# A transformer block in fp32 on TensorE: one section of the conditioning loaded earlier, block sums of the down projection split off and moved ahead, one gate/up operand made later, another order at the end

## The chip, the core and the metric

The kernel runs on one core of a Trainium2 chip. The metric is the device time of one execution in microseconds (us). Five engines work side by side, each through its own list of instructions in order: TensorE (PE, matrix products, with its weight loads as PEld), VectorE (DVE), ScalarE (ACT), GpSimd (POOL) and SyncE (SP), which here only issues DMA transfers. An instruction waits where its input is not there or its output buffer is still being read, and everything behind it on its engine waits too.

## What is computed

One block for a sequence of 1024 tokens of width 1024: a conditioning vector c gives six modulation sections; a normalised and modulated input goes through two kinds of attention, an output projection, a residual, a second modulated norm, a SwiGLU network of inner width 2816 and a last norm.

```python
mod = c_act @ w_ada[l] + b_ada[l]
sh_a, sc_a, g_a, sh_f, sc_f, g_f = jnp.split(mod[:, None, :], N_MOD, axis=-1)
h = rms_norm(x, g_mix[l]) * (1.0 + sc_a) + sh_a
x = x + g_a * hybrid_mixer(h, ...)
h = rms_norm(x, g_ffn[l]) * (1.0 + sc_f) + sh_f
x = x + g_f * swiglu(h, w_gate[l], w_up[l], w_down[l])
return rms_norm(x, g_final)
```

`swiglu` is `(silu(h @ w_gate) * (h @ w_up)) @ w_down`. The change touches the section sh_f (number 3 of six), the first block of gate/up, the down projection and the last norm.

## The kernel before

**Arithmetic.** Every fp32 product is made of three matrix products of two rounded parts: `split` (L160) lets ACT cast an operand to its high part (L162) and DVE subtract that from the operand, which is the low part (L158). In the trace these are `dhi`/`dlo`, `whi`/`wlo`, `ah`/`al`. Almost every subtraction of the kernel goes through the helper of L158, so operations are told apart by their tiles.

**Stages**, with the times at which they run in the profile: norm of x and the q/k/v projections up to 166 us; latent projections from 166 us on, and from 185 us the first attention steps between them; attention steps (`step`, the loop at L1223) to about 500 us; output projection and second norm to about 590 us; gate/up to 1022 us; down to 1243 us; the last evacuations and stores to 1255.3 us.

**What sets the order.** The code is written in the order in which each engine is to work; a scheduling layer moves instructions among their neighbours and then fixes each engine's list. Weights come through `Stream` objects (L57): an item is a load and a preparation; `pump` does the next preparation and issues loads a few items ahead, `need` and `ahead` pump up to a named item. Stream `st` feeds the stages up to the latents, `st2` output projection, gate/up and down. A third stream, `st3`, holds the eight items of section 3: each is a load of 512 KB (`adr`, L332) and one DVE operation of 128x1024 that multiplies by a number of c and accumulates (`acc`, L339 and L341); after the eighth, eight tiny matmuls (L373) turn the sum into columns, and DVE adds the bias (L383). The attention loop pumps one item of `st3` per step (L1225 to L1227). SP issues these loads in one queue with the attention's operands (`op`, L918 and L920). Working tiles share 49 slots of 4 KB per partition; a load waits in SP's queue until its slot is free.

**Gate/up** makes each block of 256 columns by seven products instead of eight (a Strassen form); `product` (L1333) is one of them, `half1` (L1280) and `rest` (L1298) make the activations' operands (`aop`: ACT cast, DVE low part) for products 6, 5, 3 and then 7, 4, and `fill` (L1331) lists what is still to be made during the first block. Operand 3 is made out of a PSUM tile, `psd`. Product 4 has weights of its own, `w4`, whose low part DVE makes last.

**Down** uses the same form over four quadrants in seven passes in the order 1, 2, 5, 6, 7, 3, 4 (`ORDER`). A pass goes through eleven items c = 0 to 10, each of 12 matmuls of 128x512 (three for each of four token tiles t). `dn_item` (L796) loads quarter blocks of g and of w_down and DVE prepares the operand: passes 1 and 2 take the blocks as they are; item ("5", c) first makes two block sums (L825 and the subtraction behind it, 128x512 each) into a tile `stt`, which passes 6, 3 and 4 use again. `ahead` (in the loop at L1469) keeps the preparations DLEAD = 3 items ahead of PE. `evac_dn` (L1419) adds a finished pass into the running results, `base21` (L1448) and `last21` (L1455) finish the last quadrant: for each t a multiplication with the gate (L1458), a subtraction from the residual x1, a square with its sum on ACT, the addition of two sums (L1462), POOL's reciprocal root (L221, L222), and the two scaled halves on ACT (L1464) and DVE (L1465), which are stored.

Of the kernel before, what the change touches and what calls it, by code (L numbers as in the profile page):

```python
# [12 lines left out]
P = 128  # L13
S = 1024
D = 1024
# [9 lines left out]
ALLOW = [(0, 'rope'), (12, ('qup', 2)), (25, None)]  # L25
# [28 lines left out]
DLEAD = 3  # L54
# [43 lines left out]
def emit(ctx, tc, a, out, dbg=None, rec=None):  # L98
# [12 lines left out]
    def slot(shape, dt, name):  # L111
        n = nm(name)
        if rec:
            rec.alloc(n)
        return sp.tile([P] + list(shape), dt, name=n, tag="s", bufs=NBUF)
# [284 lines left out]
    st.add("rope", load_tabs, lambda: None)  # L400
    for k in range(3):
        witem(st, ("qup", k), a["w_q_up"][k * P:(k + 1) * P, :], [768], nc.gpsimd)
    for k in range(2):
        witem(st, ("kvup", k), a["w_kv_up"][k * P:(k + 1) * P, :], [1024], nc.gpsimd)
    st3 = Stream(2)
    for it in col_sec(3, fin_shf):
        st3.add(*it)
# [388 lines left out]
    def dn_item(i, c):  # L796
# [5 lines left out]
        def dma():  # L802
            r = slot([2, 512], F32, "raw")
            q = None
            if i in "57":
                q = slot([2, 512], F32, "raw")
                if i == "5":
                    ld(out=r, in_=ga[:, :, HI].rearrange("f p t -> p f t"))
                    ld(out=q, in_=w0.rearrange("p (f n) -> p f n", f=2))
                else:  # L810
                    ld(out=r, in_=g0.rearrange("p (f n) -> p f n", f=2))
                    ld(out=q, in_=wa[:, :, HI].rearrange("f p t -> p f t"))
            else:
                x, y = {"1": (g0[:, LO], w0[:, LO]), "2": (g1[:, LO], w1[:, LO]), "6": (g0[:, LO], w1[:, HI]),
                        "3": (g1[:, LO], w1[:, HI]), "4": (g1[:, HI], w1[:, LO])}[i]
                ld(out=r[:, 0, :], in_=x)
                ld(out=r[:, 1, :], in_=y)
            raws[key] = (r, q)

        def prep():  # L820
            r, q = raws.pop(key)
            v = nc.vector
            if i == "5":
# [3 lines left out]
                r = z  # L827
# [81 lines left out]
    for i in ORDER:  # L909
        for c in range(NP):  # L910
            dn_item(i, c)

# [310 lines left out]
    for n in range(done, NS):  # L1223
        step(n, LA)
        if n > done:  # L1225
            st3.allow()
            st3.pump()  # L1227
        if n - NU in WOL:
            st2.need(("wo", WOL[n - NU]))
        for t in WOD.get(n - NU, []):  # L1230
            wout_d(t)
# [48 lines left out]
    def half1(jp):  # L1280
# [8 lines left out]
        if jp:  # L1289
            aop("5", jp, a11)  # L1290
        sub(nc.vector, a12, a22, a12)
        aop("3", jp, a22)
        sub(nc.gpsimd, a21, a21, t2)
        if not jp:
            aop("5", jp, a11)
# [35 lines left out]
    fill = [lambda: half1(0), lambda: half1(1)] + [lambda n=n, jp=jp: rest(n, jp) for n in "74" for jp in range(2)]  # L1331
# [123 lines left out]
    def last21(o, t):  # L1455
        t4 = 4 + t
        r = x1[t4]
        vtt(out=o, in0=o, in1=gf[:, LO], op=ALU.mult)  # L1458
        sub(nc.vector, r[:, LO], r[:, LO], o)
        sq(t4, LO, 0)  # L1460
        ss = ssq[t4]
        vtt(out=ss[:, 0:1], in0=ss[:, 0:1], in1=ss[:, 1:2], op=ALU.add)  # L1462
        rs = rstd_of(ss[:, 0:1], D)
        nc.scalar.activation(osl[t4][:, HI], r[:, HI], AF.Copy, scale=rs)  # L1464
        nc.vector.scalar_tensor_tensor(out=osl[t4][:, LO], in0=r[:, LO], scalar=rs, in1=gfin[:, LO], op0=ALU.mult, op1=ALU.mult)  # L1465
        for half in (HI, LO):
            ld(out=out[t4 * P:(t4 + 1) * P, half], in_=osl[t4][:, half])

    for n, i in enumerate(ORDER):  # L1469
# [7 lines left out]
        for c, t in seq:  # L1477
            if t == 0:
                ahead(("dn", i, c), DLEAD)
                if i in "17" and c in (2, 4, 6, 8):  # L1480
                    load_x1((c - 2) // 2 + (0 if i == "1" else 4))
# [16 lines left out]
    assert not pend  # L1498
# [54 lines left out]
```

## Time and profile before

| | us |
|---|---|
| three runs | 1255.12, 1257.43, 1259.67 (median 1257.43) |
| profiled execution | 1257.22 |
| its span | 1255.3 |
| PE busy in the span | 1205.8 (96%) |
| DVE busy | 829.2 (66%) |
| ACT busy | 494.4 (39%) |
| POOL busy | 439.0 (35%) |

The mean granted clock of TensorE was 0.983 of full speed. A row of the timeline gives the start, the duration, the engine, the line, the operation, out<-in, the shape, how many equal instructions it joins, and in brackets how long the engine sat idle before it and what ended that. A duration holds the engine's latency, so starts that follow each other without a wait are nearer together than durations: two operations of 128x512 on DVE that do not depend on each other start 0.60 us apart, though each is written as 0.68. In the page's slices 9 means nine tenths or more.

### The profile page before, as it was taken

The numbers are of one execution on the slowest core, as the hardware profiler recorded it, in microseconds if no ns is written. First come the engines' busy times: TensorE is split into PE (matmuls) and PEld (weight loads), VectorE is DVE, ScalarE is ACT, GpSimd is POOL, SyncE is SP. The second block draws the span as 40 slices with busy tenths as digits, with TensorE's granted clock in tenths as the row PEclk, the third lists the DMA queues.
The fourth block names the chain that finished last, engine by engine and source line by source line (L and its number), as shares of the span: only waits on it lengthen the run. The fifth ranks groups of instructions, "written<-read, shape, count | busy, mean of one in ns | idle before, by whom it ended". The sixth has DMA issues, their size and how long they took to land.

```text
span 1255.3 us, 16479 instructions
## 1 busy us (share of the span) xinstructions
PE 1205.8 (96%) x5951; PEld 1013.7 (81%) x5951; DVE 829.2 (66%) x1282; ACT 494.4 (39%) x850; POOL 439.0 (35%) x492
## 2 busy tenths in 40 slices
PE   8999999999899999999899999999999999999995
PEld 6888898988679898887688888878888888878774
DVE  6643514477697878768865565665555575699997
ACT  4542225455556665124532223313233244143353
POOL 4420002654243256113455445565444620000112
PEclk9999998999999999999899999999999999999998
DMA  9774842357986434321132233322122369779543
GB/s 369 301 255 167 313 137 74 106 170 227 336 250 166 137 109 144 116 94 59 51 118 96 91 117 125 110 84 84 51 101 84 117 234 393 250 252 327 190 129 135
DMA packets 82972, 209.33 MB, mean 167 GB/s; under 512 B 7805, under 2 KB 18379, under 8 KB 82763
## 3 DMA queue, kind: packets, MB, share of 16 engines
q1 hardware_dynamic: 63611, 168.36, 40.0%
q0 software_dynamic: 6336, 23.07, 4.8%
q10 hardware_dynamic: 12944, 16.84, 3.9%
q8 instruction: 47, 0.77, 0.2%
q14 instruction: 34, 0.28, 0.1%
HBM read 164.21 MB, written 44.04 MB: 166 GB/s over the span
## 4 chain that ended last, share of the span: by engine, by line
PE 77%; DVE 12%; ACT 4%; issue 4%; DMA 1%; POOL 1%; SPq 0%; ACTq 0%; POOLq 0%; DVEq 0%
PE psb L1338 32%; PE psb L439 5%; PE psb L441 5%; PE psb L440 5%; PE psb L481 3%; PE psd L481 3%; PE psd L1485 2%; PE psd L1486 2%; PE psd L1484 2%; PE psb L1030 2%; ACT s L949 2%; PE psb L1485 2%; PE psb L1484 2%; PE psb L1486 2%; DVE dlo L158 1%
## 5 line engine op out<-in xcount | busy, mean ns | idle before, releaser
L1338 PE MATMUL psb<-ah,whi 128*128 128x512 f32 x528 | 143.7, 394 | 2.9 <-ACT uv L1367 2.6
L1338 PE MATMUL psb<-ah,wlo 128*128 128x512 f32 x528 | 142.0, 391 | 0.8 <-DVE wlo L158 0.8
L1338 PE MATMUL psb<-al,whi 128*128 128x512 f32 x528 | 141.7, 390 | 0.4 <-DVE al L158 0.4
L1361 POOL TENSOR_TENSOR cf<-cf,cf 128x512 f32<-128x512 f32 x44 | 66.4, 1510 | 190.5 <-DVE cf L1354 183.9
L1338 PEld LDWEIGHTS psb<-ah,whi 128*128 128x128 f32 x528 | 99.3, 189 | 24.9 <-ACT uv L1367 3.0
L1354 DVE TENSOR_TENSOR cf<-psb,uv 128x512 f32<-128x512 f32 x88 | 60.3, 686 | 89.1 <-PE psb L1338 88.2
L1338 PEld LDWEIGHTS psb<-ah,wlo 128*128 128x128 f32 x528 | 99.6, 189 | 22.1 <-DVE wlo L158 1.2
L1338 PEld LDWEIGHTS psb<-al,whi 128*128 128x128 f32 x528 | 99.0, 188 | 21.4 <-DVE al L158 0.8
L162 ACT CAST whi<-ssum 128x1024 fp32r<-128x1024 f32 x44 | 45.0, 1045 | 166.9 <-POOL ssum L158 166.9
L158 DVE TENSOR_TENSOR wlo<-ssum,whi 128x1024 fp32r<-128x1024 f32 x44 | 62.3, 1416 | 55.5 <-ACT whi L162 55.5
L949 ACT ACTIVATE s<-s,nb 128x640 f32<-128x640 f32 (+7 forms) x96 | 74.4, 777 | 48.9 <-DVE nb L947 48.5
L162 ACT CAST dhi<-raw 128x1024 fp32r<-128x1024 f32 x63 | 64.5, 1051 | 64.5 <-DVE raw L158 29.0
L947 DVE CUSTOM_DVE_ANT_0 s<-psd,tabs 128x640 f32<-128x640 f32 (+7 forms) x80 | 63.3, 803 | 38.2 <-PE psd L973 36.1
L158 DVE TENSOR_TENSOR dlo<-raw,dhi 128x1024 fp32r<-128x1024 f32 x59 | 73.9, 1274 | 15.5 <-ACT dhi L162 15.3
L1485 PE MATMUL psb<-dlo,dhi 128*128 128x512 f32 x176 | 69.0, 392 | 0.1
L439 PE MATMUL psb<-whi,hh 128*128 128x512 f32 (+2 forms) x192 | 68.1, 354 | 1.0 <-ACT latq L638 0.9
L1486 PE MATMUL psb<-dhi,dlo 128*128 128x512 f32 x176 | 68.5, 389 | 0.0
L441 PE MATMUL psb<-whi,hl 128*128 128x512 f32 (+2 forms) x192 | 67.3, 350 | 0.0
L440 PE MATMUL psb<-wlo,hh 128*128 128x512 f32 (+2 forms) x192 | 67.2, 350 | 0.0
L1365 ACT ACTIVATE cf<-cf 128x512 f32<-128x512 f32 x44 | 27.8, 632 | 99.7 <-DVE cf L1354 99.7
L1484 PE MATMUL psb<-dhi 128*128 128x512 f32 x176 | 63.8, 391 | 1.1 <-ACT dhi L162 1.0
L1453 POOL TENSOR_TENSOR x<-x,gfin 128x512 f32<-128x512 f32 x4 | 5.5, 1377 | 164.3 <-ACT o L1417 160.0
(321 smaller groups left out, 3105.9 us busy)
## 6 DMA issues: line engine op xcount, KB each, us to landing
adr<-in_w_ada_dram SPq DMA_DIRECT2D x32, 512.0 KB, 6.4
raw<-scr_g SPq DMA_DIRECT2D x55, 256.0 KB, 3.6
raw<-in_w_down_dram SPq DMA_DIRECT2D x55, 256.0 KB, 4.2
raw<-in_w_gate_dram SPq DMA_DIRECT2D x22, 512.0 KB, 3.3
raw<-in_w_up_dram SPq DMA_DIRECT2D x22, 512.0 KB, 3.3
scr_g<-cf POOLq DMA_DIRECT2D x22, 512.0 KB, 3.2
raw<-scr_g SPq DMA_DIRECT2D x22, 512.0 KB, 5.4
raw<-in_w_down_dram SPq DMA_DIRECT2D x22, 512.0 KB, 6.2
```

The source lines that it names most:

```text
L158: pn(eng.tensor_tensor(out=o, in0=x, in1=y, op=ALU.subtract))
L162: pn(nc.scalar.copy(hi, raw))
L439: mm(o, lhsT=ah, rhs=bh, start=start, stop=False)
L440: mm(o, lhsT=ah, rhs=bl, start=False, stop=False)
L441: mm(o, lhsT=al, rhs=bh, start=False, stop=stop)
L481: pn(mm(o, lhsT=w[z == 2][:, m * 128:(m + 1) * 128], rhs=h[z == 1], start=(k == 0 and z == 0), stop=(k == 7 and z == 2)))
L949: nc.scalar.activation(s, s, AF.Exp, bias=nb[:, m:m + 1], scale=-1.0, accum_out=rs[:, m:m + 1])
L1338: mm(o, lhsT=w[l][:, k, :], rhs=x[2 * (k // 2) + r][:, k % 2, :], start=(l + r == 0 and k == 0), stop=(r == 1 and k == 3))
L1361: nc.gpsimd.tensor_tensor(out=g, in0=g, in1=o, op=ALU.mult)
L1484: mm(o[t], lhsT=hi[:, 0, tt], rhs=hi[:, 1, :], start=c == 0, stop=False)
L1485: mm(o[t], lhsT=hi[:, 0, tt], rhs=lo[:, 1, :], start=False, stop=False)
L1486: mm(o[t], lhsT=lo[:, 0, tt], rhs=hi[:, 1, :], start=False, stop=c == NP - 1)
```

## The change

1. Section 3 goes from `st3` into `st`, between the rope tables and the weights of the latents' up-projections; `st3` and its pumping are gone, and the first entry of `ALLOW` names the section's last item, so that all eight are pumped before and in the first latent projections.
2. The two block sums of down become items of their own, "s". Those of c = 0 to 5 stand after the items of passes 1 and 2 that `EARLY` names; the others directly ahead of ("5", c), which has no load of its own now. `DLEAD` is 5. The reloads of x1 go from passes 1 and 7 to passes 2 and 6.
3. In `last21` the DVE and ACT operations are pinned to the order of the code, and the second part of a tile (from the addition of the sums on) comes after the first part of the next tile.
4. In `half1` operand 5 follows operand 6 in both halves, and operand 3 is left to `fill`, which makes it after operand 7 and before operand 4.

```diff
-ALLOW = [(0, 'rope'), (12, ('qup', 2)), (25, None)]
+ALLOW = [(0, ('ad', 3, 7)), (12, ('qup', 2)), (25, None)]
...
-DLEAD = 3
+DLEAD = 5
+EARLY = [("1", 4), ("1", 7), ("1", 10), ("2", 2), ("2", 5), ("2", 8)]
...
     st.add("rope", load_tabs, lambda: None)
+    for it in col_sec(3, fin_shf):
+        st.add(*it)
     for k in range(3):
         witem(st, ("qup", k), a["w_q_up"][k * P:(k + 1) * P, :], [768], nc.gpsimd)
...
-    st3 = Stream(2)
-    for it in col_sec(3, fin_shf):
-        st3.add(*it)
...
         def dma():
+            if i == "5":
+                return
             r = slot([2, 512], F32, "raw")
             q = None
-            if i in "57":
+            if i in "s7":
...
-                if i == "5":
+                if i == "s":
                     ld(out=r, in_=ga[:, :, HI].rearrange("f p t -> p f t"))
                     ld(out=q, in_=w0.rearrange("p (f n) -> p f n", f=2))
...
-            if i == "5":
+            if i == "s":
                 z = stt[c] = slot([2, 512], F32, "stt")
                 v.tensor_tensor(out=z[:, 0, :], in0=r[:, 0, :], in1=r[:, 1, :], op=ALU.add)
                 sub(v, z[:, 1, :], q[:, 1, :], q[:, 0, :])
-                r = z
+                return
+            elif i == "5":
+                r = stt[c]
...
         for c in range(NP):
+            if i == "5" and c >= 6:
+                dn_item("s", c)
             dn_item(i, c)
+            if (i, c) in EARLY:
+                dn_item("s", EARLY.index((i, c)))
...
-        if n > done:
-            st3.allow()
-            st3.pump()
...
         aop("6", jp, t2)
-        if jp:
-            aop("5", jp, a11)
+        aop("5", jp, a11)
         sub(nc.vector, a12, a22, a12)
-        aop("3", jp, a22)
         sub(nc.gpsimd, a21, a21, t2)
-        if not jp:
-            aop("5", jp, a11)
+        sa["3", jp] = a22
         sa["4", jp] = a21
...
-    fill = [lambda: half1(0), lambda: half1(1)] + [lambda n=n, jp=jp: rest(n, jp) for n in "74" for jp in range(2)]
+    fill = [lambda: half1(0), lambda: half1(1)] + [lambda n=n, jp=jp: rest(n, jp) for n in "734" for jp in range(2)]
...
-        r = x1[t4]
-        vtt(out=o, in0=o, in1=gf[:, LO], op=ALU.mult)
-        sub(nc.vector, r[:, LO], r[:, LO], o)
-        sq(t4, LO, 0)
...
+        r, ss = x1[t4], ssq[t4]
+        pin(vtt(out=o, in0=o, in1=gf[:, LO], op=ALU.mult))
+        pin(vtt(out=r[:, LO], in0=r[:, LO], in1=o, op=ALU.subtract))
+        pin(nc.scalar.activation(osl[t4][:, LO], r[:, LO], AF.Square, accum_out=ss[:, 0:1]))
+        for fn in tail:
+            fn()
+
+        def rest():
+            pin(vtt(out=ss[:, 0:1], in0=ss[:, 0:1], in1=ss[:, 1:2], op=ALU.add))
+            rs = rstd_of(ss[:, 0:1], D)
+            pin(nc.scalar.activation(osl[t4][:, HI], r[:, HI], AF.Copy, scale=rs))
+            pin(nc.vector.scalar_tensor_tensor(out=osl[t4][:, LO], in0=r[:, LO], scalar=rs, in1=gfin[:, LO], op0=ALU.mult, op1=ALU.mult))
...
+        tail[:] = [rest]
...
-                if i in "17" and c in (2, 4, 6, 8):
-                    load_x1((c - 2) // 2 + (0 if i == "1" else 4))
+                if i in "26" and c in (2, 4, 6, 8):
+                    load_x1((c - 2) // 2 + (0 if i == "2" else 4))
```

The line numbers of the changed kernel are one higher near the top (L341 is L342), eight higher around L947 (now L955) and two higher in gate/up and down (L1354 is L1356, L1431 is L1433).

**Section 3 on DVE.** Before, among the attention steps; `ptl` is the low part of a transposed probability, the ISA operations are softmax's scaling:

```order
L341 SCALAR_TENSOR_TENSOR acc_3308<-adr_3310,cact,acc_3308 128x1024
L158 TENSOR_TENSOR ptl_3324<-psb_3381,pth_3323 128x4x128
L1000 RECIPROCAL rr_3316<-rs_3315 128x1
L158 TENSOR_TENSOR ptl_3342<-psb_3397,pth_3341 128x4x128
L1077 TENSOR_SCALAR ms_3414<-psb_3411 128x2
L341 SCALAR_TENSOR_TENSOR acc_3308<-adr_3312,cact,acc_3308 128x1024
L947 ISA s_3379,nb_3376<-psd_3390,tabs 128x768
L947 ISA nb_3376 128x1
L947 ISA s_3380,nb_3376<-psd_3404,tabs 128x768
```

In the change, behind the last low part of the values (`vl`) and ahead of the first softmax operation:

```order
L159 TENSOR_TENSOR vl_1322<-psb_1327,vh_1321 128x4x128
L340 TENSOR_SCALAR acc_1430<-adr_1388,cact 128x1024
L342 SCALAR_TENSOR_TENSOR acc_1430<-adr_1390,cact,acc_1430 128x1024
L342 SCALAR_TENSOR_TENSOR acc_1430<-adr_1392,cact,acc_1430 128x1024
L342 SCALAR_TENSOR_TENSOR acc_1430<-adr_1394,cact,acc_1430 128x1024
L342 SCALAR_TENSOR_TENSOR acc_1430<-adr_1432,cact,acc_1430 128x1024
L955 ISA s_1446,nb_1443<-psd_1447,tabs 128x128
L955 ISA nb_1443 128x1
```

Five of the eight accumulations stand together here; the other three follow in the next thirty rows.

**Gate/up, first block, on DVE.** Before, from the last low part of operand 3 (`al` out of `psd`) to w4:

```order
L158 TENSOR_TENSOR al_1293_6190<-psd_1286_6166,ah_1292_6189 128x1024
L1354 TENSOR_TENSOR cf_1280_6137<-psb_1294_6194,uv_1279_6136 128x512
L1354 TENSOR_TENSOR uv_1279_6136<-psb_1306_6245,uv_1279_6136 128x512
L158 TENSOR_TENSOR al_1296_6210<-ht_1268_6095,ah_1295_6209 128x1024
L1354 TENSOR_TENSOR uv_1279_6136<-psb_1307_6259,uv_1279_6136 128x512
L158 TENSOR_TENSOR al_1298_6214<-ht_1283_6153,ah_1297_6213 128x1024
L1354 TENSOR_TENSOR cf_1263_6075<-psb_1299_6217,uv_1262_6074 128x512
L158 TENSOR_TENSOR al_1301_6233<-ht_1229_5940,ah_1300_6232 128x1024
L158 TENSOR_TENSOR al_1303_6237<-ht_1254_6049,ah_1302_6236 128x1024
L158 TENSOR_TENSOR w4_1304_6240<-raw_1228_5938,w4_1304_6240 128x512
```

In the change, the same stretch:

```order
L1356 TENSOR_TENSOR cf_1278_6133<-psb_1290_6186,uv_1277_6132 128x512
L1356 TENSOR_TENSOR uv_1277_6132<-psb_1302_6237,uv_1277_6132 128x512
L159 TENSOR_TENSOR al_1292_6202<-ht_1268_6095,ah_1291_6201 128x1024
L1356 TENSOR_TENSOR uv_1277_6132<-psb_1303_6251,uv_1277_6132 128x512
L159 TENSOR_TENSOR al_1294_6206<-ht_1281_6149,ah_1293_6205 128x1024
L1356 TENSOR_TENSOR cf_1263_6075<-psb_1295_6209,uv_1262_6074 128x512
L159 TENSOR_TENSOR al_1297_6225<-psd_1271_6108,ah_1296_6224 128x1024
L159 TENSOR_TENSOR al_1299_6229<-psd_1284_6162,ah_1298_6228 128x1024
L159 TENSOR_TENSOR w4_1300_6232<-raw_1228_5938,w4_1300_6232 128x512
L159 TENSOR_TENSOR al_1305_6266<-ht_1229_5940,ah_1304_6265 128x1024
L159 TENSOR_TENSOR al_1307_6270<-ht_1254_6049,ah_1306_6269 128x1024
```

Operand 3's two low parts moved behind operand 7's, and operand 4's (from `ht`) from ahead of w4 to behind it.

**Down on DVE, ahead of the first evacuation of pass 7** (L1431, in the change L1433). `raw<-raw,stt` is the sum of an item of pass 3, the `dlo` of the same `raw` its low part. Before:

```order
L158 TENSOR_TENSOR raw_1969_10162<-raw_1970_10163 128x512
L158 TENSOR_TENSOR raw_1973_10186<-raw_1973_10186,stt_1844_9506 128x512
L158 TENSOR_TENSOR dlo_1976_10206<-raw_1960_10112,dhi_1975_10205 128x1024
L158 TENSOR_TENSOR dlo_1979_10227<-raw_1964_10136,dhi_1978_10226 128x1024
L158 TENSOR_TENSOR raw_1977_10209<-raw_1977_10209,stt_1849_9529 128x512
L158 TENSOR_TENSOR raw_1980_10230<-raw_1980_10230,stt_1854_9552 128x512
L158 TENSOR_TENSOR dlo_1983_10250<-raw_1969_10162,dhi_1982_10249 128x1024
L158 TENSOR_TENSOR dlo_1986_10270<-raw_1973_10186,dhi_1985_10269 128x1024
L1431 TENSOR_TENSOR uw_1766_9112<-psb_1950_10078,uw_1766_9112 128x512
```

In the change:

```order
L159 TENSOR_TENSOR dlo_1987_10248<-raw_1976_10164,dhi_1986_10247 128x1024
L159 TENSOR_TENSOR raw_1982_10210<-raw_1982_10210,stt_1808_9282 128x512
L159 TENSOR_TENSOR dlo_1990_10268<-raw_1979_10187,dhi_1989_10267 128x1024
L159 TENSOR_TENSOR raw_1985_10231<-raw_1985_10231,stt_1820_9346 128x512
L159 TENSOR_TENSOR dlo_1993_10288<-raw_1982_10210,dhi_1992_10287 128x1024
L159 TENSOR_TENSOR raw_1988_10251<-raw_1988_10251,stt_1834_9414 128x512
L159 TENSOR_TENSOR dlo_1996_10308<-raw_1985_10231,dhi_1995_10307 128x1024
L159 TENSOR_TENSOR raw_1991_10271<-raw_1991_10271,stt_1847_9481 128x512
L159 TENSOR_TENSOR dlo_1999_10328<-raw_1988_10251,dhi_1998_10327 128x1024
L1433 TENSOR_TENSOR uw_1767_9113<-psb_1962_10106,uw_1767_9113 128x512
```

One operand of pass 3 is finished ahead of the evacuation before the change, five are in the change.

## Rows read from the trace of the kernel before

**Rows 1.** The page's section 2: the span in 40 equal slices, in tenths

```profile
PE   8999999999899999999899999999999999999995
...
DVE  6643514477697878768865565665555575699997
...
PEclk9999998999999999999899999999999999999998
```

**Rows 2.** Waits of PE, longest in total: line <- releaser, us, times, longest

```profile
PE psb L988 <- DVE ptl L158: 4.2, 2, 4.0
...
PE psb L1338 <- ACT uv L1367: 2.6, 1, 2.6
...
PE psb L1338 <- DVE w L158: 2.3, 1, 2.3
```

**Rows 3.** The chain of waits, 318 to 380 us: start us, us, what

```profile
336.13 7.17 DMA adr<-in_w_ada_dram
...
343.39 1.06 DVE acc L341
...
345.33 0.69 PE psb L988
```

**Rows 4.** The timeline of SP's queue, 328 to 352 us: start, us, what

```profile
328.36 9.55 SPq L332 DMA_DIRECT2D adr<-in_w_ada_dram  x4
...
338.07 0.33 SPq L920 DMA_DIRECT2D op<-scr_qn  x1
```

**Rows 5.** The timeline of DVE, 140 to 200 us: ..., [idle before <- releaser]

```profile
166.31 0.69 DVE L158 TENSOR_TENSOR vl<-psb,vh 128x512 fp32r<-128x512 f32 x1 [4.75 <-ACT vh L459]
...
185.64 0.29 DVE L947 CUSTOM_DVE_ANT_0 s<-psd,tabs 128x128 f32<-128x128 f32 x1 [18.65 <-PE psd L973]
```

**Rows 6.** The timeline of PE, 598 to 628 us, product 4 of gate/up

```profile
622.10 1.92 PE L1338 MATMUL psb<-ah,w 128*128 128x512 f32 x4 [2.32 <-DVE w L158]
623.81 1.91 PE L1338 MATMUL psb<-al,w 128*128 128x512 f32 x4
```

**Rows 7.** The timeline of DVE, 596 to 624 us

```profile
611.13 1.21 DVE L158 TENSOR_TENSOR al<-psd,ah 128x1024 fp32r<-128x1024 f32 x1
...
616.93 3.44 DVE L158 TENSOR_TENSOR al<-ht,ah 128x1024 fp32r<-128x1024 f32 x2
...
620.29 1.75 DVE L158 TENSOR_TENSOR w<-raw,w 128x512 fp32r<-128x512 f32 x1
```

**Rows 8.** The timeline of DVE in the down projection, windows from 1078 to 1256 us

```profile
1081.58 0.70 DVE L1423 TENSOR_TENSOR psd<-psd,uw 128x512 f32<-128x512 f32 x1 [8.15 <-PE psd L1486]
1082.32 0.70 DVE L1410 TENSOR_TENSOR psd<-psd,gbc 128x512 f32<-128x512 f32 x1
...
1142.31 0.69 DVE L1428 TENSOR_TENSOR uw<-psd,uw 128x512 f32<-128x512 f32 x1 [2.00 <-PE psd L1486]
...
1172.02 0.69 DVE L1431 TENSOR_TENSOR uw<-psb,uw 128x512 f32<-128x512 f32 x1 [1.86 <-PE psb L1486]
...
1236.85 2.36 DVE L158 TENSOR_TENSOR dlo<-raw,dhi 128x1024 fp32r<-128x1024 f32 x2 [0.55 <-ACT dhi L162]
...
1240.26 1.30 DVE L1458 TENSOR_TENSOR psb<-psb,gbc 128x512 f32<-128x512 f32 x2 [1.05 <-PE psb L1486]
```

**Rows 9.** Windows: from:to, us, each engine's busy us (instructions), PEclk, DMA share, GB/s

```profile
340.00:350.00 10.00, 5.42 (x27) 5.01 (x28) 6.61 (x11) 2.99 (x8) 2.94 (x6) 0.66 1.02 404
...
1030.00:1080.00 50.00, 50.00 (x222) 41.43 (x221) 25.70 (x26) 18.14 (x20) 0.00 (x0) 1.00 1.00 368
...
1190.00:1200.00 10.00, 6.08 (x23) 3.92 (x22) 10.00 (x12) 5.07 (x7) 2.46 (x2) 0.96 0.36 117
```

**Rows 10.** The timeline of DVE at the end

```profile
1249.26 0.15 DVE L1462 TENSOR_TENSOR ssall<-ssall 128x1 f32<-128x1 f32 x1
1250.35 0.75 DVE L1465 SCALAR_TENSOR_TENSOR o<-x,rstd,gfin 128x512 f32<-128x512 f32 x1 [0.94 <-POOL rstd L222]
```

More of the change, by code (lines that the diff above doesn't have):

```diff
@@ L820, in prep @@
         def prep():
-            r, q = raws.pop(key)
+            r, q = raws.pop(key, (None, None))
             v = nc.vector
-            if i == "5":
+            if i == "s":
                 z = stt[c] = slot([2, 512], F32, "stt")
@@ L1456, in last21 @@
         t4 = 4 + t
-        r = x1[t4]
-        vtt(out=o, in0=o, in1=gf[:, LO], op=ALU.mult)
-        sub(nc.vector, r[:, LO], r[:, LO], o)
-        sq(t4, LO, 0)
[L1461 to L1467, printed above, removed]
+        r, ss = x1[t4], ssq[t4]
[9 more added lines that the diff above has]
+            pin(nc.vector.scalar_tensor_tensor(out=osl[t4][:, LO], in0=r[:, LO], scalar=rs, in1=gfin[:, LO], op0=ALU.mult, op1=ALU.mult))
+            for half in (HI, LO):
+                ld(out=out[t4 * P:(t4 + 1) * P, half], in_=osl[t4][:, half])
+        tail[:] = [rest]
+    tail = []
     for n, i in enumerate(ORDER):
@@ L1497, in emit @@
             pend += [lambda t=t: base21(t) for t in range(4)]
-    assert not pend
+    for fn in tail:
+        fn()
 _INS = ["x", "vecs", "ident", "ada_a", "ada_b", "w_ada", "b_ada", "w_in", "rope", "w_q_up", "w_kv_up", "tabs", "lam", "w_out",
```

## The prediction

> **What bounds the kernel now.** I read the page's slices first: PE stands at 9 tenths in nearly all of them, so a change pays only where PE has a hole. The holes, beside the start, are slice 11 (an 8: 314 to 345 us, attention), slice 20 (596 to 628 us, start of gate/up, with an 8 in the granted clock too) and the last; ahead of the last, DVE stands at 9 in four slices [rows 1]. The list of PE's waits then names who ends the holes: 4.2 us behind a DVE subtraction in the attention, 2.6 and 2.3 us in product line L1338 [rows 2]. Each of the four parts of the change has one of these places, and each was read in its own timeline.
>
> **Part 1, section 3.** In the chain of waits a load of `adr` runs 7.17 us, DVE's accumulation follows for 1.06, and then PE starts at 345.33 [rows 3]. PE had waited 4.0 us there [rows 2]. Nothing that PE computes at that place needs section 3: the accumulation only stands ahead of the low part of a probability in DVE's list, and DVE waits for the load. The window from 340 to 350 shows PE busy 5.42 us at a mean clock of 0.66, so part of the matmuls ran at the lower of the two levels (1.2 GHz for 2.4), with DMA at 1.02 [rows 9]. In SP's queue four `adr` loads stand from 328.36 on, over 9.55 us, ahead of an attention operand issued at 338.07 [rows 4].
>
> With the section gone from here, DVE goes straight on to the low part. The wait of 4.0 us goes, and 0.6 more of small gaps around it: -4.6. The clock: the 5.4 busy us at 0.66 would be some 3.6 at full clock, -1.9. The accumulations (eight, by the row of 1.06 some 8.5 us of DVE) are on the path only where DVE is late for PE; I estimate nothing beyond that. **-6.5**; bounds -2 (the next operand, late on a full DMA, takes over half of the wait) and -10 (4.6, 1.9 and three of the accumulations on the path).
> After a wait, PE's clock fell here: that the window stands at 0.66 is the row. The Trainium skill, "TensorE: Matmul & The Clock Gate", Part 1, says that the gate follows how busy PE has lately been, at two ratios only. By that the slow stretch stays if smaller gaps remain around the place, and the sum would be 1.9 us less negative; I take the full 1.9 since the gaps that remain are under 0.6.
>
> In its new place: DVE is idle 18.65 us up to 185.64, after the last `vl` at 166.31 [rows 5]. Five accumulations of 1.06 go there; the loads before it take slots that the first attention operands had, and these take slots which the values' projection frees from 170 on. That is over 10 us before the first softmax row, and a load took 7.17 at the worst place. Of the last three, one stands inside the first softmax chain: at most 1.06 to PE. Two stand in idle time. **+0.5**; bounds 0 and +3 (all three on the path).
>
> **Part 4, gate/up.** PE waits 2.32 us for w4's low part at 622.10, and the eight matmuls that follow start over 1.71 us per four [rows 6], where the first attention-free stretch (1030 to 1080: 222 in 50 us) gives 0.90 [rows 9]. DVE is without a gap before: the pair of low parts of product 4 takes 3.44 and w4 1.75, to 622.0 [rows 7]. The change puts that pair behind w4. Operand 3's two (1.21 each [rows 7]) stay ahead of w4 but leave the early part. So w4's low part ends about 3.4 us earlier, and PE needs it 2.3 earlier: the wait goes, -2.3. The pair that is now late is wanted after eight matmuls (1.8 us) and after ten; DVE gives it 1.2 and 2.4 us after w4: no new wait, with little to spare. The slow clock after the wait costs 2 x (1.71 - 0.90) = 1.6; I count none of it, since waits of some tenths remain around. Taking one cast of operand 3 (1.0 us, as long as the others) from ahead of ACT's copy `uv`, on which PE waits 2.6 [rows 2], gives 1.0. **-3.3**; bounds -1 (the copy alone) and -5 (with the clock).
>
> **Part 2, down.** In passes 6, 7 and 3 DVE has two sums and a low part per item. From 1190 to 1200 DVE is busy 10.00 us and PE 6.08 [rows 9]. A pass without waits takes 1172.02 - 1142.31 = 29.7 us [rows 8]; three more would end at 1231.4, but DVE's last pair of low parts starts at 1236.85 and ends at 1239.2, and PE's first result for the end comes at 1240.26 [rows 8]. So DVE sets the end, and what counts is the DVE work between 1142.31 and 1239.2 and DVE's gaps there. The gaps: 1.86 at 1172.02, where DVE waits for PE to end pass 7 with more operands to prepare behind the evacuation; 0.55 at 1236.85 [rows 8]; 1.22 of the same kind at the end of pass 3 by its timeline: 3.6. In the change five operands of pass 3 are ready ahead of that evacuation instead of one (the order above). DVE has then about 35 us of work from 1142.31 to there where PE needs 29.7, arrives after PE, and does not wait. The work: counting the rows from the first evacuation of pass 6 to the last low part in both orders, at 0.60 for an operation of 128x512 and 1.14 for a low part, 1.9 us less stand there in the change, since some were done before. **-5.4**; bounds 0 (DVE finds other gaps of the same size) and -7.8, at which PE's own 1231.4 is the limit.
>
> The cover for what moves earlier: from 1030 to 1080 DVE is busy 25.7 of 50 us [rows 9], and at 1081.58 it idles 8.15 us [rows 8]. The early sums are 6 x 1.2 = 7.2 us of DVE and 6 MB of loads in a stretch where DMA is full (1.00, 368 GB/s [rows 9]): 16 us of DMA. This window alone moved 18.4 MB. Passes 1 and 2 (22 items of 0.5 MB), the early sums, x1 (2 MB) and g_final (0.5) need 19.5 MB in all by 1081, and DLEAD lets at least five operands (2.5 MB) come before pass 1 starts, so the loads should still be ahead of PE. The x1 reloads move by a pass and cost nothing while that holds.
>
> **Part 3, the end.** Before, from 1240.26 to the end of the last row, 1250.35 + 0.75 = 1251.1: 10.8 us. Each tile needs the addition of sums, POOL's two operations and the last multiplication: 1249.26 to 1250.35, 1.09 us, in which DVE idles 0.94 [rows 10]. Before, DVE has another tile's operations in two of these four times. In the change the list reads mult, subtract (twice), then sum, multiplication, mult, subtract, sum, multiplication and so on: the sum and the multiplication that waits for it stand next to each other in all four tiles, with nothing between. A dependent pair starts 0.74 apart (1081.58 to 1082.32 [rows 8]), an independent one 0.60. So: 4 x (0.74 + 0.60) + 4 x 1.09 + 4 x 0.67 = 12.4. **+1.6**; bounds -1 (the first tile starts early, beside PE's last matmuls) and +2.5.
> The Trainium skill, "VectorE: DVE Perf Modes", The DRAIN you can't avoid, says the next operation waits for the pipeline to empty in any case, so that order among DVE operations would cost nothing; the two pitches of this trace differ, by 0.14. By the rule the end would be 4 x 0.14 = 0.6 shorter.
>
> **Sum**: -6.5 + 0.5 - 3.3 - 5.4 + 1.6 = -13.1, from the profiled execution's 1257.22: 1244.1. That execution stood 0.2 below the median of the runs, so 1244.3 against 1257.43. A difference of 0.3% (3.8 us) is about what can be told here from no change.
>
> **Rivals.**
> (a) *The attention gives little back.* DMA is full at 340 to 350 (1.02 [rows 9]); the attention operand behind the `adr` loads [rows 4] is late itself, PE waits for it, and the clock falls again. For: DMA share. Against: without 4 MB of `adr` (11 us at 368 GB/s) the operands come earlier. Then part 1 is worth -2, and the total -8.6: 1248.8.
> (b) *Down is not shortened.* DVE's gaps go, but ACT's casts, which end the gap at 1236.85 [rows 8], or the shorter lead of loads make others. Then -5.4 becomes 0, with +1.6 at the end: -7.7, 1249.7. With (a) too: 1254.
> (c) *Slower: the early sums' loads starve PE.* In the full-DMA stretch 1030 to 1080 up to six MB come ahead of pass 2's operands. If the loads are not ahead of PE as I think, PE stops in passes 2 and 5 for up to 16 us, plus some at the lower clock (as at 622.10, 1.6 each time): 16 + 3, against -13.1 + 5.4 from the rest: +11, about 1269. It decides whether the operands of pass 2 are prepared before PE comes to them; the 8.15 us of idle DVE [rows 8] speak against it.
> (d) *The change does not do what it says*: the layer that orders instructions undoes parts of it. The order shows section 3, w4 and the sums moved, so only the end (pinned) and the clock could be empty; within the range.
>
> **How the numbers follow.** The forecast's case, 1239 to 1247, has 0.58; (a) or (b) alone, 1247 to 1253, 0.24; both or smaller gains, 1253 to 1261, 0.10; (c) 0.07; the rest, faster than 1239, is 0.01. Faster by over 0.3% (below 1253.6): 0.84; within: 0.09; slower: 0.07. The range reaches from 1238 (part 1 and part 4 at their ends) to 1253 (a or b).
>
> **What would show it.** Right: no accumulation on DVE between 320 and 380, and PE's line L988 gone from its waits; five accumulations in the idle time before the first softmax row; product 4 without its wait; DVE without a gap over 0.6 from the evacuation of pass 6 to the last low part, with that low part about 5 us earlier against the start of pass 1; about 12.4 us from the first operation of the end to the last. Wrong: PE waits at DMA's operands in the attention at the same place; PE's waits in pass 2 or 5; a wait for w4's neighbours, `al` of product 4.

## The result

The changed kernel takes 1245.01 us (median of four runs, 1243.9 to 1246.36), the one before, run beside it, 1256.28 (1254.55 to 1259.67). The ratio is 0.9908, 95% interval 0.9882 to 0.9933: faster by 0.7 to 1.2%. Forecast were 1244.3 and a range of 1238 to 1253.

The page's slices of the changed kernel, in the order of [rows 1]:

```profile
PE   8999998999999999999899999999999999999994
...
DVE  6642625567777878768965565655555567598997
...
PEclk8999999999999999999999999999999999999997
```

The 8 of PE in slice 11 is gone; a new one stands in slice 7 (187 to 218 us, the latents with the first attention steps). Slice 20 keeps its 8, with the clock at 9 tenths now. The waits of PE, as in [rows 2]:

```profile
PE psd L980 <- DVE nb L955: 3.3, 4, 2.1
PE psb L1340 <- DVE al L159: 2.5, 3, 1.5
...
PE psb L1340 <- ACT ah L163: 1.8, 1, 1.8
...
PE psb L1340 <- ACT uv L1369: 1.4, 1, 1.4
```

The 4.2 us behind a probability's low part are gone; 0.9 us remain in all waits for such parts. In their place PE waits 3.3 us for softmax's scaling (L955), 3.0 of them at the first scores, and in gate/up the 2.3 us at w4 became 2.5 at low parts of activations.

To place the gain, I took from PE's and DVE's timelines the start of each stage's first matmul and the end of DVE's last operations, and compared the lengths between them. Each column below is one profiled execution, as a difference from the one of before; p1 to p4 are experiments that have one part of the change alone.

| stretch | changed | p1 | p2 | p3 | p4 |
|---|---|---|---|---|---|
| start to first q/k matmul | +1.9 | +1.8 | +1.5 | -0.2 | +1.3 |
| q/k to first `dv` matmul | 0.0 | 0.0 | +1.4 | 0.0 | +1.4 |
| to the first E by E score product | +1.5 | +1.6 | -2.6 | -2.5 | -2.7 |
| to the last E by E score product | -8.9 | -8.8 | +1.1 | +1.2 | -1.2 |
| to the first matmul of gate/up | 0.0 | 0.0 | -1.6 | 0.0 | 0.0 |
| gate/up | -1.1 | 0.0 | -0.2 | 0.0 | -0.9 |
| down, to the end of DVE's last low part | -6.3 | 0.0 | -6.3 | 0.0 | -1.3 |
| from there to DVE's last operation | +1.7 | 0.0 | +0.1 | +1.6 | 0.0 |
| span | -11.3 | -5.7 | -6.7 | +0.1 | -3.5 |

The E by E products are those of L988, the first of which follows the latents and the last of which lies in the attention. In the first rows also p2 to p4 differ, which do not touch those stages: there the same instructions take up to 2.7 us more or less by chance. In these profiles the rows of gate/up and of the end repeat to 0.3 us, and so does down but for p4.

### The profile page after: what moved, and what is told of

Same layout as the page of the kernel before. It is cut to its first block, busy times and chain, and to the rows that moved or that the text cites. A ratio compares the mean times of both kernels' runs of the same rounds, so it can differ in the third digit from the quotient of the medians.

```text
span 1244.0 us, 16493 instructions
## 1 busy us (share of the span) xinstructions
PE 1198.6 (96%) x5951; PEld 1011.3 (81%) x5951; DVE 828.8 (67%) x1282; ACT 495.5 (40%) x850; POOL 438.1 (35%) x492
## 4 chain that ended last, share of the span: by engine, by line
PE 79%; DVE 12%; issue 3%; ACT 3%; DMA 1%; POOL 1%; SPq 0%; ACTq 0%; POOLq 0%; DVEq 0%
PE psb L1340 32%; PE psb L439 5%; PE psb L441 5%; PE psb L440 5%; PE psb L481 3%; PE psd L481 3%; PE psb L1493 2%; PE psb L1494 2%; PE psb L1492 2%; PE psb L1038 2%; DVE dlo L159 2%; PE psd L1494 2%; PE psd L1493 2%; PE psd L1492 2%; ACT s L957 1%
## 5 line engine op out<-in xcount | busy, mean ns | idle before, releaser
L1356 DVE TENSOR_TENSOR cf<-psb,uv 128x512 f32<-128x512 f32 x88 | 60.3, 686 | 91.2 <-PE psb L1340 90.2
L955 DVE CUSTOM_DVE_ANT_0 s<-psd,tabs 128x640 f32<-128x640 f32 (+7 forms) x80 | 63.3, 804 | 28.6 <-PE psd L981 26.8
```

## Experiments

**One part alone**, each on the kernel before.

```diff
# p1_section: part 1
+    for it in col_sec(3, fin_shf):
+        st.add(*it)
...
# p2_down: part 2
+DLEAD = 5
+EARLY = [("1", 4), ("1", 7), ("1", 10), ("2", 2), ("2", 5), ("2", 8)]
...
# p3_end: part 3
...
+        tail[:] = [rest]
# p4_gate: part 4
+        aop("5", jp, a11)
...
+        sa["3", jp] = a22
...
```

> The kernel before with part 1 alone (section 3 loaded ahead of the latent up-projections). Theory: the attention gets shorter by 8.9 us between its first score product of the second kind and its last score, as between the two traces, and the latents longer by 1.4: about 7.5 us less than before. Rival: the accumulations' new place costs as much as the prediction's upper bound, or the attention's gain needs the other parts: 2 to 4 us less.

Measured: 1250.34 us, ratio 0.9956 (0.9939 to 0.9972). -8.8 in the attention and +1.6 ahead of it, as in the changed kernel: by the profiles the theory holds, and the rest of the change has no part in it. The medians differ by 4.9 us only (interval 3.5 to 7.7); what may lie between is told under no_section.

> The kernel before with part 2 alone (block sums as items, six of them early, five items of lead, x1 reloads in passes 2 and 6), old end. Theory: DVE without gaps after pass 6, last matmul 7.8 us earlier against the first of down: about 7.8 us less than before. Rival: the old end, whose DVE operations are mixed with the last preparations, loses as much as it gains: 3 to 5 us less.

Measured: 1250.17 us, ratio 0.9952 (0.9931 to 0.9972). The last matmul comes 7.8 us earlier against the first of down, as the theory says, but DVE's last low part, from which the end follows, only 6.3: PE finishes 2.2 us after that low part where it took 3.7. So the stretch that counts is 6.3 us shorter. The medians differ by 5.1 us, with an interval of 3.5 to 8.7 that holds theory and rival.

> The kernel before with part 3 alone (the pinned order at the end). Theory: DVE waits for POOL's two operations four times instead of two and a half: from the first operation of the end to the last 12.5 us instead of 10.8, about 1.6 us more than before. Rival: the new order is what lets the last matmuls end earlier against DVE's last low part (2.3 us instead of 3.8 between the two traces): no change, or 1 us less.

Measured: 1257.37 us, ratio 1.0014 (0.9994 to 1.0034). The runs cannot tell it from no change; the profile can: 1.6 us more between DVE's last low part and its last operation, and no other stretch that the part touches differs.

> The kernel before with part 4 alone (operand 3 made later). Theory: DVE is the bound in the first block of gate/up, and product 4 waits for its own low parts in place of w4: 1 to 1.3 us less than before, as between the two traces. The prediction's step: 3.3 us less.

Measured: 1252.97 us, ratio 0.9976 (0.9956 to 0.9996). Gate/up is 0.9 us shorter, 1.1 in the changed kernel: by the profiles the theory, not the prediction's 3.3; the interval of the runs, 0.5 to 5.5 us, holds both. (Of the 3.5 us of its span, the rest lies in stretches it does not touch.)

**The end in other orders**, on the changed kernel.

```diff
# old_end: the end as before
-        pin(vtt(out=o, in0=o, in1=gf[:, LO], op=ALU.mult))
+        vtt(out=o, in0=o, in1=gf[:, LO], op=ALU.mult)
...
# new_end: a tile's sum, then its scaled halves, each one tile later
-        for fn in tail:
-            fn()
...
+        if len(tail) == 2:
+            tail.pop(0)()
+        if tail:
+            tail[0] = tail[0]()
+        tail.append(total)
...
```

> The changed kernel with the old end (parts 1, 2 and 4). Theory: the pinned end costs 1.6 us here too, as when it stood alone: 1.6 us less than the changed kernel. Rival: with part 2 the old end's operations collide with the last preparations, and the pinned end is needed: no difference, or slower than the changed kernel.

Measured: 1243.39 us (1242.95 to 1245.69), ratio 0.9903 (0.9877 to 0.9928); the profile has 1.6 us less than the changed kernel in the stretch of the end, and the same down (-6.3). By the profile the theory holds; by the runs the interval overlaps with the changed kernel's.

> The changed kernel with a third order at the end: a tile's sum goes to POOL after the next tile's first part, and its scaled halves come after the first part of the tile after that, so that POOL's 1.1 us lie beside DVE's work. Theory: POOL's way is what the end waits for; from the first operation of the end to the last some 9.4 us where the changed kernel takes 12.5 and the one before 10.8: 3 us less than the changed kernel. Rival: the end is bound by ACT's squares and copies: 1 us less at most.

Measured: 1242.61 us (1242.32 to 1244.45), ratio 0.9896 (0.9872 to 0.9921). DVE's timeline at the end:

```profile
1228.35 0.69 DVE L1460 TENSOR_TENSOR psb<-psb,gbc 128x512 f32<-128x512 f32 x1
...
1231.01 0.15 DVE L1465 TENSOR_TENSOR ssall<-ssall 128x1 f32<-128x1 f32 x1
1231.08 0.69 DVE L1460 TENSOR_TENSOR psb<-psb,gbc 128x512 f32<-128x512 f32 x1
...
1232.41 0.74 DVE L1470 SCALAR_TENSOR_TENSOR o<-x,rstd,gfin 128x512 f32<-128x512 f32 x1
...
1236.24 0.75 DVE L1470 SCALAR_TENSOR_TENSOR o<-x,rstd,gfin 128x512 f32<-128x512 f32 x1 [0.73 <-POOL rstd L223]
1237.71 0.75 DVE L1470 SCALAR_TENSOR_TENSOR o<-x,rstd,gfin 128x512 f32<-128x512 f32 x1 [0.72 <-POOL rstd L223]
```

10.1 us from the first row to the end of the last, against 12.5 in the changed kernel and 10.8 before. The multiplication at 1232.41 follows its sum without a wait, because another tile's first part lies between; only the last two wait for POOL. Expected were 9.4: the third and fourth sums stand together, and POOL works them off one after the other. The interval of the runs overlaps with the changed kernel's here too.

**Section 3 in and out of its new place**, on the changed kernel.

```diff
# late_three
-ALLOW = [(0, ('ad', 3, 7)), (12, ('qup', 2)), (25, None)]
+ALLOW = [(0, ('ad', 3, 4)), (6, ('ad', 3, 7)), (12, ('qup', 2)), (25, None)]
# no_section
-ALLOW = [(0, ('ad', 3, 7)), (12, ('qup', 2)), (25, None)]
+ALLOW = [(0, 'rope'), (12, ('qup', 2)), (25, None)]
...
-    for it in col_sec(3, fin_shf):
-        st.add(*it)
+    nc.vector.tensor_copy(fcol[:, 1, :], V[:, 32:40])
```

> The changed kernel with the last three items of section 3 allowed six steps later, so that their accumulations stand behind the first unit's softmax instead of inside it. Theory: these three, each 1.28 us on DVE, keep back the first scores, on which PE waits 3.3 us in the changed kernel: from the values' projection to the first score of the second kind 2 to 4 us less, the attention unchanged. Rival: the latents' longer time comes from the order of the score products themselves or from the clock, not from these three: no difference.

Measured: 1244.91 us (1244.31 to 1246.09), ratio 0.9913 (0.9892 to 0.9935): the changed kernel's time. In the profile the stretch up to the first E by E product is 1.2 us longer than in the changed kernel and the attention 1.3 shorter. The accumulations did hold PE up: between 186 and 222 us it waits 1.3 us behind L955 where it waited 3.0. But its wait for ACT's `latq` at L669, 0.3 us in the changed kernel, is 2.1 now, so that its waits in that stretch come to 3.9 against 3.8, and the clock stood lower than the changed kernel's 0.88 (below):

```profile
186.00:200.00 14.00, 11.23 (x51) 9.78 (x50) 7.83 (x26) 8.23 (x24) 2.10 (x7) 0.76 0.14 38
```

So the theory falls as to what the move is worth: with the three out of the way, another wait stands in their place.

> The changed kernel with section 3 left out (its columns hold the bias alone; no loads, no accumulations), to bound what its place can cost. Theory: the latents lose the whole price of the new place, 2 to 4 us less than the changed kernel up to the first score of the second kind, and the attention is as in the changed kernel. Rival: the place is free but for chance: within 1 us of the changed kernel.

Measured: 1242.72 us (1239.27 to 1243.12), ratio 0.9888 (0.9862 to 0.9915). Its stretch from the first `dv` matmul to the first E by E product has the length of the kernel before (+0.1), 1.4 less than the changed kernel's; the attention is as in the changed kernel (-8.6). So the new place costs 1.4 us by the profiles and 2.3 by the medians, whose intervals overlap. Followed from matmul to matmul against the kernel before, PE of the changed kernel falls back by 0.9 us at the first scores and by 1.0 more where the section's tiny matmuls now stand, among the latents; 0.4 come back later. In the kernel before they stood in the attention. The kernel before, then the changed one:

```profile
374.85 2.05 PE L373 MATMUL psb<-ones,acc 128*128 128x1 f32 x16
```

```profile
216.41 1.84 PE L374 MATMUL psb<-ones,acc 128*128 128x1 f32 x16
```

What blurs the price is PE's clock behind the first scores, which the window from 186 to 200 us shows, here in the kernel before,

```profile
186.00:200.00 14.00, 11.48 (x52) 10.52 (x51) 7.40 (x24) 8.08 (x24) 2.12 (x7) 0.76 0.13 38
```

in p3_end, where the code of this stage is the same,

```profile
186.00:200.00 14.00, 11.46 (x69) 10.46 (x68) 8.92 (x29) 9.72 (x29) 3.04 (x10) 1.00 0.26 75
```

and in the changed kernel:

```profile
186.00:200.00 14.00, 10.09 (x50) 8.49 (x49) 8.71 (x25) 7.45 (x22) 2.09 (x7) 0.88 0.49 119
```

With the same busy time and the same waits (1.6 and 0.9 us), PE gets through 52 or 69 records, because the granted clock fell or did not: that is the 2.5 to 2.7 us by which p2, p3 and p4 are shorter there. It makes the price of the new place anything from 1.4 (the clock fell in both) to 4 us (against p2 to p4). From 186 to 220 us the clock stood at 1.00 in four of the six profiles that have section 3 in its old place and at 0.90 in two; in all seven that have it in the new place it stood at 0.90 or 0.95. So the higher price may well be the more frequent one, and with it the stretches of p1 would come to 4.7 us, near the 4.9 of its runs; single profiles do not show it.

**Lead and sums apart**, on the kernel before.

```diff
# lead_only
-DLEAD = 3
+DLEAD = 5
# sums_only
...
+            if (i, c) in EARLY:
+                dn_item("s", EARLY.index((i, c)))
```

> The kernel before with DLEAD 5 alone: the block sums stay in item 5. Theory: the longer lead alone puts more operands of pass 3 ahead of the evacuation of pass 7, so that DVE's waits at the pass ends go: from the first matmul of down to DVE's last low part 3 to 4 us less of the 6.3 that part 2 gives. Rival: without sums made in the idle time of passes 1 and 2 the lead cannot be filled: under 1 us.

Measured: 1248.75 us, ratio 0.995 (0.9926 to 0.9974). Down to DVE's last low part is 5.0 us shorter: more than either theory said. But DVE's waits at the ends of passes 6 and 7 did not go. DVE in lead_only at the evacuations of passes 6 and 7:

```profile
1142.88 0.69 DVE L1428 TENSOR_TENSOR uw<-psd,uw 128x512 f32<-128x512 f32 x1 [2.34 <-PE psd L1486]
...
1172.12 0.69 DVE L1431 TENSOR_TENSOR uw<-psb,uw 128x512 f32<-128x512 f32 x1 [2.51 <-PE psb L1486]
```

They are 2.34 and 2.51, against 2.00 and 1.86 [rows 8]. What the lead gives is that more operands are finished when DVE arrives there: from the evacuation of pass 6 to the end of the last low part DVE is busy 2.9 us less, and idle 1.1 us less, since the waits at the end of pass 3 and ahead of the last low parts (1.22 and 0.55 in the kernel before) are gone. The other 0.9 us come at the end of pass 5 (below).

> The kernel before with the block sums as items of their own, six of them early, but DLEAD 3 and the x1 reloads as before. Theory: the six sums (7 us of DVE) leave the stretch only up to pass 6, where DVE still waits for PE at the evacuation; behind that DVE's list is the same and the gain is under 1 us of the 6.3. Rival: the sums are what shortens DVE's work: 4 us or more.

Measured: 1253.74 us, ratio 0.999 (0.9968 to 1.0012), no difference by the runs. The profile has down 2.2 us shorter to DVE's last low part, with the waits as before (2.33 and 1.87). Lead and sums add up to 7.1 apart and give 6.3 together, as the 0.9 us at the end of pass 5 are in both; p2_down also moves the reloads of x1, which was not tried alone. The wait at pass 7 is gone only with both, as in p2_down, whose one remaining wait is this:

```profile
1140.91 1.29 DVE L1437 TENSOR_TENSOR uw<-psd,uw 128x512 f32<-128x512 f32 x2 [6.04 <-PE psd L1495]
```

**Gate/up's first block and a last kernel**, on the changed kernel.

```diff
# pool_seven; both_new has it too
     def rest(n, jp):
-        aop(n, jp, sa[n, jp])
+        hi, lo = A[n, jp] = (slot([2, 512], F32R, "ah"), slot([2, 512], F32R, "al"))
+        split(sa[n, jp], hi, lo, nc.gpsimd if n == "7" else None)
# both_new, the end: first parts of all tiles ahead of the third sum
...
+        if 0 < t < 3:
+            tail[-1] = tail[-1]()
+        tail.append(total)
...
```

> The changed kernel with the two low parts of operand 7 made on POOL, which idles then, in place of DVE. Theory: the first block of gate/up is bound by the sum of DVE's work: 2.4 us of it go, and gate/up gets 1.5 to 2.2 us shorter. Rival: POOL and DVE slow each other where both work between tiles (the low part of operand 6 takes 2.4 us beside POOL's subtraction, others 1.2): no gain, or up to 1 us longer.

Measured: 1245.67 us (1244.55 to 1246.99), ratio 0.9919 (0.9889 to 0.9949); gate/up is 0.2 us longer than in the changed kernel. The rival holds, and by more than this: in the changed kernel the clock falls behind product 4's waits, here it does not (next section), and no_section, where it does not either, has gate/up 1.2 us shorter than this. DVE's timeline there, and POOL's:

```profile
601.77 3.41 DVE L159 TENSOR_TENSOR al<-ht,ah 128x1024 fp32r<-128x1024 f32 x1
```

```profile
601.36 2.73 POOL L159 TENSOR_TENSOR al<-ht,ah 128x1024 fp32r<-128x1024 f32 x1 [0.60 <-ACT ah L163]
```

A subtraction that takes DVE 1.21 us alone takes 3.41 beside POOL's: the 2.4 us that DVE gave away come back as slower work.

> The changed kernel with operand 7's low parts on POOL and a fourth order at the end, in which all four first parts come before the third and fourth sums. Theory: the end takes 9.0 us from its first operation to the last (third order: 10.1, changed kernel: 12.5), so that with the gain of POOL's part about 1239.5 to 1240.5. Rival: without a gain from POOL's part, 1241.5.

Measured: 1243.2 us (1242.15 to 1246.86), ratio 0.9903 (0.9873 to 0.9934). The end takes 9.9 us from its first operation to the last, 0.2 less than in new_end, not 1.1: the last two tiles still wait for POOL, 0.65 and 0.71 us. With no gain from POOL's part it is not better than new_end, which has the lowest median of a kernel that computes everything; their intervals overlap.

## Why the prediction was right, and where it was not

**Section 3, attention** (forecast -6.5, measured -8.9 between the profiles). The wait and the clock were as worked out. The window from 340 to 350 us of the changed kernel, against [rows 9]:

```profile
340.00:350.00 10.00, 9.75 (x75) 9.31 (x75) 8.00 (x21) 7.06 (x19) 2.43 (x8) 1.00 0.92 289
```

9.75 us busy at full clock for 5.42 at 0.66. By the start of the first L988 product after the wait 4.5 us are gained (4.6 forecast), by 351 us another 1.8 (1.9 forecast, 1.8 by its own rows). With the wait gone the clock stayed at 1.00, as the prediction took it. The step that was mis-sized is "I estimate nothing beyond that" for the accumulations: 2.5 us more are gained between 351 and 359 us of the kernel before. There one of them stands ahead of a softmax scaling on which PE then waits. The kernel before:

```profile
354.52 1.27 DVE L341 SCALAR_TENSOR_TENSOR acc<-adr,cact,acc 128x1024 f32<-128x1024 f32 x1
```

```profile
356.46 0.44 PE L1030 MATMUL psb<-ident,s 128*128 128x128 f32 x2 [0.87 <-DVE nb L947]
```

In this stretch PE idles 1.3 us before the change and not at all after it. The three accumulations that follow and the tiny matmuls at 374.85 gave nothing more in this profile: from there to the last E by E product both kernels take the same time; the changed kernel waits 1.28 us for another DVE result in that stretch. That the whole gain comes from moving section 3 p1 shows; that it is this accumulation which gave the 2.5 us is read from the rows, not tried alone.

**Section 3, new place** (+0.5; measured +1.4 to +1.5, its price open up to 4). The bound of +3 held for the profiles compared. DVE's timeline in the changed kernel:

```profile
168.75 0.74 DVE L340 TENSOR_SCALAR acc<-adr,cact 128x1024 f32<-128x1024 f32 x1
...
169.53 5.25 DVE L342 SCALAR_TENSOR_TENSOR acc<-adr,cact,acc 128x1024 f32<-128x1024 f32 x4
...
188.75 0.29 DVE L955 CUSTOM_DVE_ANT_0 s<-psd,tabs 128x128 f32<-128x128 f32 x1 [13.97 <-PE psd L981]
...
191.58 1.28 DVE L342 SCALAR_TENSOR_TENSOR acc<-adr,cact,acc 128x1024 f32<-128x1024 f32 x1
...
193.85 1.28 DVE L342 SCALAR_TENSOR_TENSOR acc<-adr,cact,acc 128x1024 f32<-128x1024 f32 x1
```

Five lie in the idle time, as forecast, with 13.97 us of it left; each takes 1.2 us, not the 1.06 that I read from the chain. The two at 191.58 and 193.85 stand between softmax operations, and 3.0 of PE's 3.3 us at L980 are there; I had priced one of them. They do hold PE up, but late_three, which puts them behind, is no faster, since ACT's `latq` is waited for instead. The tiny matmuls, 1.84 us of PE among the latents, I had put at nothing. How the price divides between these and the clock stays open.

**Gate/up** (-3.3, measured -1.1). The failed step is "no new wait, with little to spare". w4's low part is early, as forecast, and the eight matmuls with it run on, but then PE waits twice, 0.69 and 1.48. This is a sign of being wrong that the prediction names, a wait for `al` of product 4:

```profile
612.09 1.98 PE L1340 MATMUL psb<-ah,w 128*128 128x512 f32 x8
614.76 0.74 PE L1340 MATMUL psb<-al,w 128*128 128x512 f32 x2 [0.69 <-DVE al L159]
616.98 1.22 PE L1340 MATMUL psb<-al,w 128*128 128x512 f32 x2 [1.48 <-DVE al L159]
```

DVE's list and POOL's at that time say why:

```profile
611.39 1.09 DVE L159 TENSOR_TENSOR w<-raw,w 128x512 fp32r<-128x512 f32 x1
612.40 4.52 DVE L159 TENSOR_TENSOR al<-ht,ah 128x1024 fp32r<-128x1024 f32 x2
```

```profile
613.59 2.26 POOL L159 TENSOR_TENSOR ssum<-raw,raw 128x512 f32<-128x512 f32 x1
615.81 2.26 POOL L159 TENSOR_TENSOR ssum<-raw,ssum 128x512 f32<-128x512 f32 x1
```

I had taken the pair at 1.2 and 2.4 us behind w4. It took 4.52, with POOL's sums beside it; the rows of the kernel before already showed a pair at 3.44 [rows 7], where 1.21 each would make 2.4, and w4 at 1.75, which takes 1.09 here. So product 4 gives nothing: 2.32 us of waiting became 2.17.

The 1.1 us that are left come ahead of it. The wait for ACT's copy `uv` did fall from 2.6 to 1.4, and the clock, which fell behind it in the kernel before (0.89 in 590 to 606 us), stayed at 1.00: 2.6 us are gained there. A wait for ACT's `ah` takes 1.5 of them back:

```profile
600.99 0.72 PE L1340 MATMUL psb<-ah,whi 128*128 128x512 f32 x2 [1.76 <-ACT ah L163]
```

Behind product 4's waits the clock fell again in both kernels. What that costs no_section shows, in whose profile the waits in gate/up are the same and the clock holds: its gate/up is 2.1 us shorter than before, not 1.1. The changed kernel, then no_section:

```profile
610.00:630.00 20.00, 17.82 (x71) 13.87 (x70) 18.21 (x18) 7.33 (x10) 14.12 (x9) 0.91 0.16 53
```

```profile
610.00:630.00 20.00, 17.70 (x75) 13.69 (x75) 17.57 (x17) 6.36 (x8) 15.31 (x9) 1.00 0.16 53
```

**Down** (-5.4, measured -6.3, and 5.4 of it as worked out). DVE's timeline in the changed kernel, the evacuations of passes 2 and 6 and the last low part:

```profile
1074.90 0.70 DVE L1425 TENSOR_TENSOR psd<-psd,uw 128x512 f32<-128x512 f32 x1 [12.77 <-PE psd L1494]
...
1134.74 1.29 DVE L1430 TENSOR_TENSOR uw<-psd,uw 128x512 f32<-128x512 f32 x2 [6.06 <-PE psd L1494]
...
1225.04 1.23 DVE L159 TENSOR_TENSOR dlo<-raw,dhi 128x1024 fp32r<-128x1024 f32 x1
```

Between the last two, no row of DVE has a wait; PE waits twice:

```profile
1146.11 0.50 PE L1493 MATMUL psb<-dlo,dhi 128*128 128x512 f32 x1 [0.98 <-DVE dlo L159]
...
1225.06 1.20 PE L1492 MATMUL psb<-dhi 128*128 128x512 f32 x4 [0.62 <-ACT dhi L163]
```

From 1134.74 to the low part's end at 1226.27 are 91.5 us, where the kernel before took 1239.2 - 1142.31 = 96.9: 5.4 less, the 3.6 of gaps and 1.8 of work (1.9 forecast; its two terms make 5.5, which it writes as 5.4). The other 0.9 come ahead of the evacuation of pass 6: at the end of pass 5, from 1108 to 1112, PE of the kernel before ran with small holes, which the forecast did not name. DVE idles 6.06 us there and 12.77 at pass 2, so nothing was short: rival (c) asked for the opposite. lead_only corrects the reading, though. I had put the lead's gain down to the gaps; with the lead alone the gaps of passes 6 and 7 stay, and most of the gain is work done ahead of them.

**The end** (+1.6, measured +1.7): 12.47 us, 12.4 forecast. The sum and the multiplication behind it, with POOL's way between, as in [rows 10] but in all four tiles:

```profile
1227.37 0.69 DVE L1460 TENSOR_TENSOR psb<-psb,gbc 128x512 f32<-128x512 f32 x1
...
1230.04 0.15 DVE L1467 TENSOR_TENSOR ssall<-ssall 128x1 f32<-128x1 f32 x1
1231.13 0.75 DVE L1470 SCALAR_TENSOR_TENSOR o<-x,rstd,gfin 128x512 f32<-128x512 f32 x1 [0.94 <-POOL rstd L223]
...
1239.09 0.75 DVE L1470 SCALAR_TENSOR_TENSOR o<-x,rstd,gfin 128x512 f32<-128x512 f32 x1 [0.94 <-POOL rstd L223]
```

The pitches were as in the kernel before: 0.73 within a dependent pair, 0.60 after it. The end's 12.47 agree with these pitches. The Trainium skill's sentence that the next operation waits for the pipeline to empty ("VectorE: DVE Perf Modes", The DRAIN you can't avoid) does not tell the two apart; the trace does, by 0.13.

**The sum.** Forecast -13.1, measured -11.3 between the profiles, of which +1.9 came in the first 18 us, ahead of any changed instruction. Without that it is -13.2: attention 2.4 and down 0.9 better than forecast, gate/up 2.2 and the new place 1.0 worse, the end 0.1. Two errors of some 2 us cancelled, so the sum is closer than its terms, by luck. Of the rivals, (a) and (c) asked for operands that come late, and neither trace nor runs show one: DMA is still at 0.92 in the window above, and PE does not wait for it there. (b) asked for other gaps of DVE in down, and there are none behind the evacuation of pass 6.

## What to carry to other kernels

Look for work that stands in an engine's list ahead of something the bounding engine waits for, but is itself not needed there: moving it earlier, into measured idle time, gave the largest part here, and more than its longest wait alone. Price the place it goes to as well, with all that goes along: here 1.4 to 4 us came back as waits, as tiny matmuls and as a lower clock. Before counting on an engine finishing an operation in time, take the duration from rows in which its neighbour works as it will then. At a short serial tail, order so that another tile's work lies between a request to a far engine and its answer; the change did the opposite, at 1.7 us, and an order that does so got 2.4 back.

## What the runs showed that was not expected

DVE and POOL slow each other heavily in some pairs of operations and not at all in others. DVE's 128x1024 subtraction took 1.21 us alone, 2.26 each beside POOL's sums, 3.41 beside POOL's subtraction of the same form; POOL's sums of 128x512 took 2.26 each there. Giving POOL 2.4 us of DVE's work gained nothing. But where DVE's input came out of PSUM (`psd`), in the changed kernel at 609.13, neither lost anything:

```profile
609.13 2.34 DVE L159 TENSOR_TENSOR al<-psd,ah 128x1024 fp32r<-128x1024 f32 x2
```

```profile
610.63 1.30 POOL L880 TENSOR_TENSOR ssum<-raw 128x512 f32<-128x512 f32 x1
```

And one profiled execution is a thin sample where PE's clock hangs on a wait: between 186 and 200 us the same instruction lists ran at a granted clock of 0.76 or 1.00, which is 2.5 to 2.7 us of the kernel's time.
